# First norm's sums of squares by rows, and the first pair's values in turn with its keys and queries

## The chip, the cores and the metric

The kernel runs on one core of one Trainium2 chip. The metric is the device time of one execution in microseconds (us); the kernel before takes 1274.79 us, the median of three runs from 1274.36 to 1276.12. TensorE is called PE here, VectorE DVE, ScalarE ACT, GpSimd POOL, and SyncE SP; SP issues nearly all DMA transfers and does so in the order of its queue.

## What is computed

One layer of a hybrid encoder trunk on 1024 tokens and 16 learned meta tokens ahead of them, 1040 rows of 1024 features:

```python
def rmsnorm(x, g):
    y = x32 * lax.rsqrt(jnp.mean(x32 * x32, axis=-1, keepdims=True) + EPS)
    return y * g
a = rmsnorm(h, norm1)
proj = a @ w_in                     # pooling input, FoX q/k/v, forget gates, stick-breaking q/k/v
y_pool = multiscale_pool_mixer(u)   # windows 2, 4, 8, 16
y_fox = forgetting_attention(qf, kf, vf, log_f)      # 6 heads of 64, causal softmax with a gate bias
y_sb = stick_breaking_attention(qs, ks, vs)          # 6 heads of 64, strictly causal
h = h + concat(y_pool, y_fox, y_sb) @ w_out
a = rmsnorm(h, norm2)
h = h + (silu(a @ w_gate) * (a @ w_up)) @ w_down
out = rmsnorm(h, final_norm)[16:]
```

All of it is float32. The kernel splits each operand into a high part that PE reads in its fast float32 format and a low part (the rest), and makes three matmuls of each product: high by high, low by high, high by low.

## The kernel before, in words

The head of the program, the first 60 us, is what the change touches. The tokens lie in memory twice: transposed (`xT`, features on the 128 partitions, eight tiles of 1040 tokens) and by rows (`xtok`, used later for the residual).

The loop over the eight tiles (L206) loads a transposed tile, splits it into high and low parts scaled by the norm's gain (L219 on ACT, L220 on DVE), and multiplies it with the first weights: the queries and the keys of the first pair of heads, which add up over the eight tiles in five PSUM buffers ("o" and "s"). The weights come in parts of 128 KB; POOL makes the high part and DVE the low one (L163 to L167). The scale of each token, one over the root of its mean square, isn't known yet; it is multiplied in later, when a product leaves PSUM.

For that scale, `square` (L198) squares each tile on ACT and adds it to an accumulator, on POOL for tiles 1, 3 and 5 and on DVE for the other four. After the loop the accumulator is split, and PE sums it over the partitions with a matrix of ones (L236 to L238), which leaves each token's sum on all partitions at once. ACT makes the scale `rbc` [128, 1040] of it (L242, L244). Two of the three sums lie in the PSUM buffers "mm", of which there are two.

`project_first` then makes the first pair ready: `queries` for both halves of the tokens (scale on DVE at L307, the high part on POOL, its copy to the other half of the partitions on ACT at L314, the low part on DVE at L315), `keys` for three ranges of tokens (L319, a high part on POOL, L327), and last `values`. That is a generator: it loads its weights, and for each of three ranges of tokens makes 24 matmuls into an "mm" buffer (L292), scales the result on DVE (L357), and turns it by PE into another "mm" buffer (`turn`, L343), from which ACT and DVE write the high and low parts (L350, L351). It gives way at two places within the 24 matmuls, at their end, and after each `turn`.

After that the attention of six pairs runs in turn with a stream of filler: the projections of the next pairs, the pooling mixer, and the output projection. The first pair is a stick-breaking one; its scores (L449 to L454) start with the last queries and the last keys, and a softmax-like chain on ACT and DVE follows (L481 to L494).

The order of instructions on each engine is not the written one. A planner simulates the engines and takes what is ready by priority; the written order is the priority, and attention gets 300 places of advance. Buffers of one name are taken in rotation in the written order, so a tile waits for the release of the one that had its buffer before.

Of the kernel before, what the change touches and what calls it, by code (L numbers as in the profile page):

```python
# [8 lines left out]
F32 = mybir.dt.float32  # L9
F32R = mybir.dt.float32r  # L10
BF16 = mybir.dt.bfloat16
AF = mybir.ActivationFunctionType
ALU = mybir.AluOpType
PSUM = bass.MemoryType.PSUM

D = 1024
KD = 8
NM = 16
SEQ = 1024
L = NM + SEQ  # L20
# [3 lines left out]
NB = 9  # L24
T0 = 528
KPIECES = ((0, 264), (264, 264), (528, 512))
# [4 lines left out]
def hymba_trunk(  # L31
# [19 lines left out]
    nc = tc.nc  # L51
    V, S, G, PE = nc.vector, nc.scalar, nc.gpsimd, nc.tensor

    def pool(name, side=None, space=None, bufs=1):
        kw = {}
        if side is not None:
            kw["side"] = side
        if space is not None:
            kw["space"] = space
        return tc.tile_pool(name=name, bufs=bufs, reuse_waits="tile", **kw)  # L60
# [3 lines left out]
    def T(p, shape, dt, tag, bufs=1):  # L64
        uid[0] += 1
        return p.tile(list(shape), dt, tag=tag, bufs=bufs, name=f"{tag}_{uid[0]}")
# [9 lines left out]
    def hi_pool(o, i):  # L76
        G.tensor_scalar(o, i, 1.0, 0.0, ALU.mult, ALU.add)
# [13 lines left out]
    def mm(tag, shape, bufs):  # L91
        return T(ps, shape, F32, tag, bufs)

    MMB, SB_, OB = 2, 4, 2
# [6 lines left out]
    sp_ = st_stack.enter_context(pool("st"))  # L101
# [6 lines left out]
    identr = cst.tile([128, 128], F32R, name="identr")  # L108
# [16 lines left out]
    epst = cst.tile([128, 1], F32, name="epst")  # L125
# [26 lines left out]
    V.tensor_copy(hmean[0:64, 0:64], tmp4[0:64, 0:64])  # L152
    V.tensor_copy(hmean[64:128, 64:128], tmp4[64:128, 64:128])

    ones = T(sp_, [128, 128], F32R, "ones")
    tmp5 = T(sp_, [128, 128], F32, "c3")
    V.memset(tmp5, 1.0)
    V.tensor_copy(ones, tmp5)


    def wpart(c, hf):
        raw = T(r1, [128, 2, 128], F32, "wr", 4)
        nc.sync.dma_start(raw, w_in[c, :, 2 * hf:2 * hf + 2, :])  # L163
        wh = T(r1, [128, 2, 128], F32R, "wh", WB)
        hi_pool(wh, raw)
        wl = T(r1, [128, 2, 128], F32R, "wl", WB)
        WPE[0].tensor_tensor(wl, raw, wh, ALU.subtract)  # L167
        return wh, wl
# [12 lines left out]
    def xhi(k, t0, n):  # L181
        if t0 < T0:
            return xs["h0", k // 2][:, k % 2, t0:t0 + n]
        return xs["h1", k // 2][:, k % 2, t0 - T0:t0 - T0 + n]
# [5 lines left out]

    first_q = [mm("o", [128, 512], OB) for _ in range(2)]
    first_k = [mm("s", [128, 512], SB_) for _ in range(3)]
    sums = [mm("s", [128, 512], SB_)] + [mm("mm", [128, 512], MMB) for _ in range(2)]
    C0 = PAIRS[0][1]
    acc = T(sp_, [128, L], F32, "acc")
    raws = {}

    def square(k):  # L198
        if k == 0:
            S.activation(acc, raws[k], AF.Square)  # L200
            return
        sq = T(sp_, [128, L], F32, "sq", 2)
        S.activation(sq, raws[k], AF.Square)
        (G if k in (1, 3, 5) else V).tensor_tensor(acc, acc, sq, ALU.add)

    for k in range(KD):  # L206
        raws[k] = T(sp_, [128, L], F32, "xr", 4)
        nc.sync.dma_start(raws[k], xT[:, k, :])
        if k % 2 == 0:
            wq = wpart(C0, k // 2)  # L210
            wk = wpart(C0 + 3, k // 2)
        if k % 2 == 0:
            xs["h0", k // 2] = T(x0, [128, 2, T0], F32R, "xa", 4)
            xs["h1", k // 2] = T(hp, [128, 2, 512], F32R, "x1", 8)
            xs["l1", k // 2] = T(hp, [128, 2, 512], F32R, "x1", 8)
        xs["l0", k] = T(x0, [128, T0], F32R, "xb", 8)
        for t0, n in ((0, T0), (T0, 512)):
            rw = raws[k][:, t0:t0 + n]
            S.activation(xhi(k, t0, n), rw, AF.Copy, scale=n1[:, k:k + 1])  # L219
            V.scalar_tensor_tensor(xlo(k, t0, n), rw, n1[:, k:k + 1], xhi(k, t0, n), ALU.mult, ALU.subtract)  # L220
        if k >= 2:
            square(k - 2)
        for ww, xx in ((0, xhi), (0, xlo), (1, xhi)):
            st, sp2 = k == 0 and (ww, xx) == (0, xhi), k == KD - 1 and ww == 1
            for j in range(2):
                PE.matmul(first_q[j], wq[ww][:, k % 2, :], xx(k, NM + 512 * j, 512),
                          start=st, stop=sp2)
            for i, (t0, n) in enumerate(KPIECES):
                PE.matmul(first_k[i][:, :n], wk[ww][:, k % 2, :], xx(k, t0, n), start=st, stop=sp2)
    square(KD - 2)  # L230
    square(KD - 1)
    sqh = T(sp_, [128, L], F32R, "sqh")
    S.copy(sqh, acc)
    sql = T(sp_, [128, L], F32R, "sq", 2)
    V.tensor_tensor(sql, acc, sqh, ALU.subtract)
    for i, (t0, n) in enumerate(KPIECES):  # L236
        PE.matmul(sums[i][:, :n], ones, sqh[:, t0:t0 + n], start=True, stop=False)
        PE.matmul(sums[i][:, :n], ones, sql[:, t0:t0 + n], start=False, stop=True)  # L238

    rbc = T(r1, [128, L], F32, "rbc")  # L240
    for i, (t0, n) in enumerate(KPIECES):
        S.activation(rbc[:, t0:t0 + n], sums[i][:, :n], AF.Ln, scale=1.0 / D, bias=epst[:, 0:1])  # L242
    for t0, n in KPIECES:
        S.activation(rbc[:, t0:t0 + n], rbc[:, t0:t0 + n], AF.Exp, scale=-0.5)  # L244


    csum = T(r1, [128, L], F32R, "csum")
# [57 lines left out]
    def queries(pr, j, p):  # L305
        t = T(at, [128, 512], F32, "pt", 3)
        V.scalar_tensor_tensor(t, p, 0.125, rbc[:, NM + 512 * j:NM + 512 * j + 512], ALU.mult, ALU.mult)  # L307
        first = pr is prs[0]
        for h in range(2):
            a, b = 64 * h, 64 * (1 - h)  # L310
            hi, lo = pr.q1[h][j], pr.q2[h][j]
            zero_r(G, lo[b:b + 64, :])
            hi_pool(hi[a:a + 64, :], t[a:a + 64, :])
            S.copy(hi[b:b + 64, :], t[a:a + 64, :])  # L314
            (V if first or h else G).tensor_tensor(lo[a:a + 64, :], t[a:a + 64, :], hi[a:a + 64, :], ALU.subtract)  # L315

    def keys(pr, t0, n, p):
        t = T(at, [128, 512], F32, "pt", 3)
        V.tensor_tensor(t[:, :n], p[:, :n], rbc[:, t0:t0 + n], ALU.mult)  # L319
        for h in range(2):  # L320
            a, b = 64 * h, 64 * (1 - h)
            src = t[a:a + 64, :n]
            dh = pr.k1[h][a:a + 64, t0:t0 + n]
            dl = pr.k1[h][b:b + 64, t0:t0 + n]
            first = pr is prs[0]
            hi_pool(dh, src)
            (V if first else G).tensor_tensor(dl, src, dh, ALU.subtract)  # L327

    def values(pr, cv):
        w = wload(cv)  # L330
        pr.v = [T(at, [128, NB, 128], F32R, "v", 4) for _ in range(2)]

        for h in range(2):
            zero_r(G, pr.v[h][:, 0, :])

        todo = None

        def turn(t, b0, nb):
            tp = mm("mm", [128, 4, 128], MMB)
            c = 0  # L340
            for i in range(nb):
                m = NM if b0 + i == 0 else 128
                PE.transpose(tp[:m, i, :], t[:, c:c + m], ident)  # L343
                c += m
            for i0, rows, ni in (((0, NM, 1), (1, 128, 2)) if b0 == 0 else ((0, 128, nb),)):
                for h in range(2):
                    src = tp[:rows, i0:i0 + ni, 64 * h:64 * h + 64]
                    dh = pr.v[h][:rows, b0 + i0:b0 + i0 + ni, 64 * h:64 * h + 64]
                    dl = pr.v[h][:rows, b0 + i0:b0 + i0 + ni, 64 - 64 * h:128 - 64 * h]
                    S.copy(dh, src)  # L350
                    V.tensor_tensor(dl, src, dh, ALU.subtract)  # L351

        for t0, n, b0, nb in ((0, NM + 256, 0, 3), (NM + 256, 256, 3, 2), (T0, 512, 5, 4)):
            o = []
            yield from proj_piece(w, t0, n, o)
            t = T(at, [128, 512], F32, "pt", 3)
            V.tensor_tensor(t[:, :n], o[0][:, :n], rbc[:, t0:t0 + n], ALU.mult)  # L357
            if todo is not None:
                turn(*todo)
                yield 0.5  # L360
            todo = (t, b0, nb)
        turn(*todo)
        yield 0.5
# [20 lines left out]
    def project_first(pr, c):  # L384
        forget_weights()
        new_queries(pr)
        for j in (1, 0):
            queries(pr, j, first_q[j])
        new_keys(pr)
        for i, (t0, n) in enumerate(KPIECES):  # L390
            keys(pr, t0, n, first_k[i])
        for _ in values(pr, c + 6):
            pass


# [470 lines left out]
    g = len(OGROUPS) - 1  # L866
# [157 lines left out]
    for c0 in range(2, FF, 2):  # L1024
# [6 lines left out]
        for key, x in up.items():  # L1031
            g = gate[key]
# [61 lines left out]
    for k, (n, direct_, to) in enumerate(DOWN):  # L1094
        ps_ = [mm("s", [128, 512], SB_) if k % 2 == 0 else mm(("mm", "o")[b // 2], [128, 512], 2) for b in range(4)]
        for c0 in range(2, FF, 2):
            x = loaded(lsd[n, c0], "sg")
            if direct_:
                i, dh = direct_
# [91 lines left out]
```

## Time and profile before

| | |
|---|---|
| median of the runs | 1274.79 us |
| profiled execution | 1275.25 us |
| its span, first to last instruction | 1273.5 us |
| busy PE, DVE, ACT, POOL | 95%, 72%, 49%, 38% |
| mean granted clock of PE | 0.987 |
| moved by DMA | 147.12 MB, 116 GB/s on average |

The profile is of one execution. The busy time of an engine is a sum over its instructions; a stage's row says how much of that stage each engine was busy. The granted clock is the share of its full speed that PE was given. In a row of waits, `A <- B` means that an instruction of A sat idle until B was done. In a row of the timeline the first number is the start and the second the duration in us.

### The profile page before, as it was taken

How to read it: one execution, taken by the hardware profiler on the slowest of the kernel's cores; microseconds unless marked ns; L12 is line 12 of the kernel's file. 1: busy time of each engine (PE TensorE's matmuls, PEld its weight loads, DVE VectorE, ACT ScalarE, POOL GpSimd, SP SyncE). 2: the span in 40 equal slices, each digit the busy share in tenths (PEclk: the TensorE clock that was granted, in tenths of full speed). 3: DMA queues.
4: the chain of work that ended last, by engine and by line, in shares of the span. 5: the costliest groups of instructions: out<-in, count | busy, mean ns of one | idle time of the engine just before them, and what ended most of it. 6: DMA issues, size and time to landing. Idle time of an engine off the chain costs nothing.

```text
span 1273.5 us, 18419 instructions
## 1 busy us (share of the span) xinstructions
PE 1214.7 (95%) x6358; PEld 1024.5 (80%) x6358; DVE 916.6 (72%) x1576; ACT 623.6 (49%) x1270; POOL 486.5 (38%) x546
## 2 busy tenths in 40 slices
PE   7799899999999989999999999999999999999997
PEld 5588688889888877787787888888888888788885
DVE  8668975657857678998687676666676646766557
ACT  6466754545538677778644232333232324344443
POOL 6459245463355774440105445334354310000001
PEclk9899999999999999999999999999999999999999
DMA  5100011010101161201514554444554448576653
GB/s 181 42 13 29 15 49 33 30 38 18 51 28 32 38 229 54 75 26 66 190 67 133 190 180 160 147 142 133 190 186 155 153 142 310 170 224 194 194 174 141
DMA packets 73146, 147.12 MB, mean 116 GB/s; under 512 B 9053, under 2 KB 21341, under 8 KB 73053
## 3 DMA queue, kind: packets, MB, share of 16 engines
q1 hardware_dynamic: 69728, 142.01, 33.9%
q10 hardware_dynamic: 3324, 3.95, 0.9%
q8 instruction: 50, 0.82, 0.3%
q14 instruction: 44, 0.35, 0.1%
HBM read 103.98 MB, written 41.94 MB: 115 GB/s over the span
## 4 chain that ended last, share of the span: by engine, by line
PE 70%; DVE 15%; issue 5%; ACT 5%; DMA 3%; POOL 1%; DVEq 0%; SPq 0%; POOLq 0%; ACTq 0%
PE s L901 22%; PE mm L292 12%; PE mm L901 8%; PE s L1086 7%; PE mm L712 4%; PE o L533 4%; DVE r L490 3%; PE s L544 3%; PE o L1086 3%; PE mm L1086 3%; DVE P L492 1%; PE s L449 1%; PE s L451 1%; DVE pl L548 1%; DVE x L714 1%
## 5 line engine op out<-in xcount | busy, mean ns | idle before, releaser
L901 PE MATMUL s<-t,wh 128*128 128x512 f32 x544 | 168.8, 389 | 1.6 <-ACT wh L887 1.6
L901 PEld LDWEIGHTS s<-t,wh 128*128 128x128 f32 x544 | 101.9, 188 | 23.4 <-ACT wh L887 2.2
L901 PE MATMUL s<-s,wh 128*128 128x512 f32 x384 | 118.5, 390 | 0.9 <-ACT wh L887 0.9
L548 DVE TENSOR_TENSOR pl<-s,ph 128x512 fp32r<-128x512 f32 (+1 forms) x168 | 92.3, 569 | 36.3 <-ACT ph L547 32.2
L887 ACT CAST wh<-ss 128x512 fp32r<-128x512 f32 x80 | 49.6, 622 | 127.2 <-PE s L901 92.2
L547 ACT CAST ph<-s 128x512 fp32r<-128x512 f32 (+1 forms) x168 | 79.2, 495 | 60.2 <-PE o L533 32.7
L901 PE MATMUL s<-t,wl 128*128 128x512 f32 x272 | 105.6, 389 | 0.0
L292 PE MATMUL mm<-x,wh 128*128 128x512 f32 (+1 forms) x320 | 100.7, 388 | 0.4 <-DVE pt L357 0.4
L1074 ACT CAST wh<-sg 128x512 fp32r<-128x512 f32 x74 | 46.1, 624 | 108.0 <-PE s L1086 43.0
L901 PE MATMUL mm<-t,wh 128*128 128x512 f32 x320 | 98.6, 389 | 0.0
L1075 DVE TENSOR_TENSOR wl<-sg,wh 128x512 fp32r<-128x512 f32 x74 | 51.1, 691 | 60.4 <-ACT wh L1074 60.2
L887 ACT CAST wh<-raw 128x512 fp32r<-128x512 f32 x68 | 41.8, 622 | 106.0 <-PE s L901 67.3
L544 PE MATMUL s<-identr,P 128*128 128x128 f32 x528 | 81.7, 275 | 6.3 <-DVE pl L548 2.3
L901 PEld LDWEIGHTS s<-s,wh 128*128 128x128 f32 x384 | 72.0, 188 | 16.2 <-ACT wh L887 1.3
L1125 POOL TENSOR_TENSOR r<-r,mhalf 128x1 f32<-128x1 f32 x8 | 4.4, 550 | 210.7 <-DVE r L1124 209.1
L533 PE MATMUL o<-pl,v 128*128 128x256 f32 (+1 forms) x288 | 81.6, 308 | 0.6 <-DVE pl L548 0.6
L995 DVE TENSOR_TENSOR cg<-s,tmp 128x512 f32<-128x512 f32 x60 | 41.3, 688 | 55.5 <-PE s L901 55.4
L292 PE MATMUL mm<-xa,wh 128*128 128x264 f32 (+3 forms) x248 | 77.4, 314 | 1.0 <-ACT rbc L242 0.7
L533 PE MATMUL o<-ph,v 128*128 128x256 f32 (+1 forms) x288 | 76.9, 283 | 0.1
L292 PE MATMUL mm<-xb,wh 128*128 128x264 f32 (+3 forms) x248 | 76.7, 311 | 0.0
L292 PE MATMUL mm<-xa,wl 128*128 128x264 f32 (+3 forms) x248 | 76.4, 312 | 0.0
L544 PEld LDWEIGHTS s<-identr,P 128*128 128x128 f32 x528 | 62.0, 140 | 16.8 <-DVE pl L548 4.5
(290 smaller groups left out, 3574.8 us busy)
## 6 DMA issues: line engine op xcount, KB each, us to landing
sg<-lsd SPq DMA_DIRECT2D x70, 256.0 KB, 3.3
raw<-in_w_gate SPq DMA_DIRECT2D x22, 512.0 KB, 5.3
raw<-in_w_up SPq DMA_DIRECT2D x22, 512.0 KB, 3.7
wr<-in_w_in SPq DMA_DIRECT2D x80, 128.0 KB, 2.2
raw<-in_w_down SPq DMA_DIRECT2D x20, 512.0 KB, 3.6
lsd<-cg SPq DMA_DIRECT2D x40, 256.0 KB, 3.4
raw<-rsd SPq DMA_DIRECT2D x40, 256.0 KB, 3.3
raw<-in_w_down SPq DMA_DIRECT2D x34, 256.0 KB, 3.1
```

The source lines that it names most:

```text
L292: PE.matmul(p[:, :n], w[k][ww], xx(k, t0, n), start=i == 0, stop=i == 23)
L533: PE.matmul(po[:, c:256], pr.v[h][:, kb, :], x, start=first and ix == 0, stop=(kb == nkb - 1 and ix == 1), skip_group_check=True)
L544: PE.transpose(tp[:, 128 * i:128 * i + 128], ptiles[ii][:, k0:k0 + 128], ident)
L547: S.copy(ph[:, :n], tp[:, :n])
L548: V.tensor_tensor(pl[:, :n], tp[:, :n], ph[:, :n], ALU.subtract)
L712: PE.matmul(p, y_[:, ts_], w_[:, ds], start=i == 0, stop=i == 3 * len(ws) - 1)
L887: S.copy(wh, a)
L901: PE.matmul(p, ws[ww][:, k, :], xs_[xx][:, k, :], start=first and i == 0, stop=i == 11, skip_group_check=True)
L995: V.tensor_tensor(t, x, y, ALU.add)
L1074: S.copy(wh, a)
L1075: V.tensor_tensor(wl, a, wh, ALU.subtract)
L1086: PE.matmul(p, x[xx][:, 128 * b:128 * b + 128], y[yy], start=first and i == 0, stop=last and i == 2, skip_group_check=True)
```

## The change

The sums of squares are taken from `xtok` instead. Nine blocks of 128 tokens (the last has 16) are loaded by rows, 512 KB each, through four buffers; ACT squares a block and sums along its rows in one instruction, so that each token's sum is one number on its own partition, in a tile `ssq1` [128, 9]. Rows 0 to 5 are loaded from tile 2 of the loop on, each behind that tile's own load, and the squares follow two tiles later. The scale is made on those nine columns. To spread it over all partitions it is split into a high and a low part, and PE multiplies, for each block, the column broadcast as a weight with the identity: 18 matmuls, into one "s" and two "mm" buffers, and three copies to `rbc`. The matrix of ones, the accumulator and its additions go.

In `project_first` the values no longer come last. A piece of them (three steps of the generator) stands behind the upper queries, behind each of the three key ranges, now from the last to the first, and then come the lower queries and the rest. The high parts of the first pair's keys go from POOL to ACT.

```diff
-    ones = T(sp_, [128, 128], F32R, "ones")
...
-    sums = [mm("s", [128, 512], SB_)] + [mm("mm", [128, 512], MMB) for _ in range(2)]
-    acc = T(sp_, [128, L], F32, "acc")
-    def square(k):
-        if k == 0:
-            S.activation(acc, raws[k], AF.Square)
-            return
-        sq = T(sp_, [128, L], F32, "sq", 2)
-        S.activation(sq, raws[k], AF.Square)
-        (G if k in (1, 3, 5) else V).tensor_tensor(acc, acc, sq, ALU.add)
+    ssq1 = T(sp_, [128, NB], F32, "ssq1")
+    V.memset(ssq1, 1.0)
+    def load_rows(r):
+        n = min(128, L - 128 * r)
+        rows[r] = T(sp_, [128, D], F32, "xk", 4)
+        nc.sync.dma_start(rows[r][:n, :], xtok[128 * r:128 * r + n, :])
+    def square(r):
+        n = min(128, L - 128 * r)
+        S.activation(rows[r][:n, :], rows[r][:n, :], AF.Square, accum_out=ssq1[:n, r:r + 1])
...
         if k >= 2:
-            square(k - 2)
+            load_rows(k - 2)
+        if k >= 4:
+            square(k - 4)
...
-    square(KD - 2)
-    square(KD - 1)
-    sqh = T(sp_, [128, L], F32R, "sqh")
-    S.copy(sqh, acc)
-    sql = T(sp_, [128, L], F32R, "sq", 2)
-    V.tensor_tensor(sql, acc, sqh, ALU.subtract)
-    for i, (t0, n) in enumerate(KPIECES):
-        PE.matmul(sums[i][:, :n], ones, sqh[:, t0:t0 + n], start=True, stop=False)
-        PE.matmul(sums[i][:, :n], ones, sql[:, t0:t0 + n], start=False, stop=True)
+    for r in range(KD - 4, NB):
+        if r >= KD - 2:
+            load_rows(r)
+        square(r)
+    S.activation(ssq1, ssq1, AF.Ln, scale=1.0 / D, bias=epst[:, 0:1])
+    S.activation(ssq1, ssq1, AF.Exp, scale=-0.5)
+    rrh = T(sp_, [128, NB], F32R, "rrh")
+    V.tensor_copy(rrh, ssq1)
+    rrl = T(sp_, [128, NB], F32R, "rrl")
+    V.tensor_tensor(rrl, ssq1, rrh, ALU.subtract)
     rbc = T(r1, [128, L], F32, "rbc")
-    for i, (t0, n) in enumerate(KPIECES):
-        S.activation(rbc[:, t0:t0 + n], sums[i][:, :n], AF.Ln, scale=1.0 / D, bias=epst[:, 0:1])
-    for t0, n in KPIECES:
-        S.activation(rbc[:, t0:t0 + n], rbc[:, t0:t0 + n], AF.Exp, scale=-0.5)
+    for g in range(3):
+        p = mm("s", [128, 512], SB_) if g == 0 else mm("mm", [128, 512], MMB)
+        blocks = range(4 * g, min(4 * g + 4, NB))
+        for r in blocks:
+            n = min(128, L - 128 * r)
+            c = 128 * (r - 4 * g)
+            for x in (rrh, rrl):
+                PE.matmul(p[:, c:c + n], x[:, r:r + 1].to_broadcast([128, 128]), identr[:, :n],
+                          start=x is rrh, stop=x is rrl, skip_group_check=True)
+        n = c + n
+        (S.copy if g != 1 else V.tensor_copy)(rbc[:, 512 * g:512 * g + n], p[:, :n])
...
-            hi_pool(dh, src)
+            (S.copy if first else hi_pool)(dh, src)
...
     def project_first(pr, c):
         forget_weights()
         new_queries(pr)
-        for j in (1, 0):
-            queries(pr, j, first_q[j])
         new_keys(pr)
-        for i, (t0, n) in enumerate(KPIECES):
-            keys(pr, t0, n, first_k[i])
-        for _ in values(pr, c + 6):
+        vals = values(pr, c + 6)
+
+        def piece():
+            for _ in range(3):
+                next(vals, None)
+
+        queries(pr, 1, first_q[1])
+        piece()
+        for i in (2, 1, 0):
+            keys(pr, *KPIECES[i], first_k[i])
+            piece()
+        queries(pr, 0, first_q[0])
+        for _ in vals:
             pass
```

More of the change, by code (lines that the diff above doesn't have):

```diff
@@ L153, in hymba_trunk @@
     V.tensor_copy(hmean[64:128, 64:128], tmp4[64:128, 64:128])
-    ones = T(sp_, [128, 128], F32R, "ones")
-    tmp5 = T(sp_, [128, 128], F32, "c3")
-    V.memset(tmp5, 1.0)
-    V.tensor_copy(ones, tmp5)
     def wpart(c, hf):
@@ L192, in hymba_trunk @@
     first_k = [mm("s", [128, 512], SB_) for _ in range(3)]
-    sums = [mm("s", [128, 512], SB_)] + [mm("mm", [128, 512], MMB) for _ in range(2)]
     C0 = PAIRS[0][1]
-    acc = T(sp_, [128, L], F32, "acc")
-    raws = {}
-    def square(k):
-        if k == 0:
-            S.activation(acc, raws[k], AF.Square)
-            return
-        sq = T(sp_, [128, L], F32, "sq", 2)
-        S.activation(sq, raws[k], AF.Square)
-        (G if k in (1, 3, 5) else V).tensor_tensor(acc, acc, sq, ALU.add)
+    ssq1 = T(sp_, [128, NB], F32, "ssq1")
+    V.memset(ssq1, 1.0)
+    raws, rows = {}, {}
+    def load_rows(r):
[5 more added lines that the diff above has]
+        S.activation(rows[r][:n, :], rows[r][:n, :], AF.Square, accum_out=ssq1[:n, r:r + 1])
     for k in range(KD):
```

## The prediction, made before the result

> **What bounds the kernel now.** I read the page's busy times first, then busy time by stage, then who waited for whom on TensorE (PE), and last the timeline of the first 60 us, since every edit lies there.
>
> ```profile
> span 1273.5 us, 18419 instructions
> PE 1214.7 (95%) x6358; PEld 1024.5 (80%) x6358; DVE 916.6 (72%) x1576; ACT 623.6 (49%) x1270; POOL 486.5 (38%) x546
> ```
>
> PE is busy for 1214.7 of 1273.5 us, so 59 us is all that reordering can win. The next view cuts the span where PE's work changes: the first queries and keys (to 34.82), the norm (to 39.84), the first two value pieces (to 47.46), a hole (to 50.70), the third value piece (to 57.26), and then attention. Columns: length, then busy time and instruction count of PE, PE's weight load, DVE, ACT and POOL, then the granted clock, DMA share and GB/s.
>
> ```profile
> 0.00:34.82 34.82, 25.36 (x119) 21.18 (x120) 30.36 (x45) 19.60 (x25) 21.73 (x40) 1.00 0.54 173
> 34.82:39.84 5.02, 1.89 (x10) 0.94 (x8) 3.08 (x4) 2.06 (x4) 2.36 (x3) 1.00 0.19 58
> 39.84:47.46 7.62, 7.61 (x48) 7.40 (x48) 5.89 (x9) 4.05 (x8) 4.76 (x7) 0.78 0.10 32
> 47.46:50.70 3.24, 0.00 (x1) 0.01 (x1) 3.08 (x7) 0.00 (x0) 1.57 (x3) 0.93 0.00 0
> 50.70:57.26 6.56, 6.56 (x25) 5.38 (x25) 2.84 (x7) 0.94 (x4) 3.50 (x7) 0.78 0.07 21
> 57.26:70.00 12.74, 9.88 (x58) 8.54 (x57) 10.10 (x18) 9.29 (x22) 1.70 (x3) 0.87 0.10 32
> 70.00:140.00 70.00, 65.64 (x416) 55.74 (x415) 53.79 (x93) 47.27 (x109) 49.52 (x54) 1.00 0.08 24
> 500.00:1273.50 773.50, 754.23 (x3437) 620.60 (x3435) 551.17 (x788) 325.26 (x588) 213.54 (x161) 0.99 0.47 154
> ```
>
> From 70 us on PE is busy for 65.64 of 70 and later 754.23 of 773.5: work that reaches PE earlier in the head ends earlier at the end. In the head PE loses 9.5 us in the first stage, 3.1 in the norm, 3.2 in the hole, 2.9 in early attention; and the clock of 0.78 in two stages costs 0.22 x 7.62 = 1.7 and 0.22 x 6.56 = 1.4 us more. PE's own waits (total us, times, longest):
>
> ```profile
> PE o L226 <- POOL wh L77: 7.3, 1, 7.3
> PE mm L343 <- DVE pt L357: 3.8, 2, 3.3
> PE s L449 <- DVE P L492: 2.3, 1, 2.3
> PE o L226 <- DVE xb L220: 2.0, 1, 2.0
> PE s L237 <- ACT sqh L233: 1.4, 1, 1.4
> PE s L238 <- DVE sq L235: 1.1, 1, 1.1
> PE mm L292 <- ACT rbc L242: 0.7, 1, 0.7
> ```
>
> The first is the load of the first weights and stays. The 2.0, and the 1.4 + 1.1 + 0.7 = 3.2 of the norm, and the hole (3.3) are what the change touches. The timeline shows why DVE was late for the 2.0 (start, duration):
>
> ```profile
> 18.20 2.53 POOL L204 TENSOR_TENSOR acc<-acc,sq 128x1040 f32<-128x1040 f32 x1 [2.27 <-DVE c L157]
> 18.39 2.92 DVE L220 SCALAR_TENSOR_TENSOR xb<-xr,n,xa 128x528 fp32r<-128x528 f32 x1
> 22.03 0.76 DVE L220 SCALAR_TENSOR_TENSOR xb<-xr,n,xa 128x528 fp32r<-128x528 f32 x1
> ```
>
> The same DVE instruction takes 0.76 us alone and 2.92 beside POOL's addition of squares: it stands still until POOL is done.
>
> **What goes, and what DVE gets back.**
>
> ```profile
> L204 POOL TENSOR_TENSOR acc<-acc,sq 128x1040 f32<-128x1040 f32 x3 | 8.2, 2742 | 4.8 <-ACT x L219 2.5 <-DVE c L157 2.3
> L204 DVE TENSOR_TENSOR acc<-acc,sq 128x1040 f32<-128x1040 f32 x4 | 4.9, 1232 | 0.0
> ```
>
> Gone are four DVE additions (4.9 us), the three POOL additions with up to 2.92 - 0.76 = 2.2 us of stall each on DVE (some 6.5), the copy and split of the accumulator, six matmuls and six wide ACT passes. DVE was busy for 30.4 of 34.8 us and loses about 11. Then PE's own work sets the first stage: it ends 2.0 + 0.2 us earlier, at about 33 rather than 35.2. That does not by itself move anything: the value matmuls need two PSUM buffers ("mm") that the norm holds first, before and after.
>
> **What comes instead: when the last row lands.** Nine loads by rows join SP's queue, 8 x 0.524 + 0.066 = 4.26 MB, as much as the eight transposed tiles (8 x 0.532 = 4.26) beside 1.05 MB of first weights. In all 9.6 MB must land. What DMA gave:
>
> ```profile
> 2.00:14.00 12.00, 6.74 (x23) 5.74 (x24) 8.67 (x13) 8.63 (x14) 9.80 (x21) 1.00 0.98 318
> 14.00:30.00 16.00, 13.99 (x75) 11.69 (x73) 15.96 (x23) 8.71 (x13) 8.41 (x9) 1.00 0.38 118
> xr<-in_xT SPq DMA_DIRECT2D x8, 520.0 KB, 4.5
> ```
>
> Full, it moves 318 GB/s; from 14 us it stood at 0.38, because tiles came free late. If it stays full from 2 us, 9.6/0.318 = 30.2 us: the last row lands at 32.2, or 33.8 if the 0.5 MB of value weights slip ahead. The queue order lets it stay nearly full: SP can have four transposed tiles and four rows under way; row 4 waits for the square of row 0, written after tile 4's copies, and so on to row 7, which waits for the square of row 3, after tile 7's copies. Tile 7 lands at 2 + 7.9/0.318 = 27, its copies and square 3 end at about 29.5; row 7, issued then, lands about 4 us later (4.5 is the median under load). I take **33 us** for the last row. Behind the waiting rows in SP's in-order queue stand tile 7 (needed by PE at about 30, so there with 3 us to spare) and the value weights (needed at 40). Bounds: 31 (row 7 issued with tile 7's landing, 4 us more) and 40.6 (after 14 us only the mean of the two rates, 218 GB/s, for the remaining 5.8 MB).
>
> [...] The trace's own 318 over 12 full microseconds is used here.
>
> **From the last row to the value matmuls.** The nearest rows for the new small steps:
>
> ```profile
> L737 ACT ACTIVATE xa<-x x8: 1042/1054/1062, 591.6 to 627.5; 128x1024 f32<-128x1024 f32 x8
> L737 ACT ACTIVATION_READ_ACCUMULATOR xa<-x x8: 183/186/192, 592.5 to 628.4; 128x1 f32 x8
> L739 ACT ACTIVATE r<-ssq,epst x4: 280/291/297, 592.8 to 603.4; 128x1 f32<-128x1 f32 x4
> L740 ACT ACTIVATE r<-r x4: 199/203/206, 593.1 to 603.7; 128x1 f32<-128x1 f32 x4
> L1124 DVE TENSOR_SCALAR r<-ssq x7: 144/144/148, 1250.5 to 1266.1; 128x1 f32<-128x1 f32 x7
> 96.51 0.44 PE s L544 x4
> ```
>
> A square with its sum is 1.05 + 0.19 = 1.24 us; ACT has room for nine (11 us; it was busy for 19.6 of 34.8, of which 8 x 1.06 squares go). After the last row: two squares less the 0.2 between the two landings, 2.2; Ln and Exp on nine columns 0.5; two tiny DVE steps 0.3; handovers 0.4: 3.4 us. Then 18 matmuls with 128 moving columns, of which 16 lie before the second group's copy: at 0.11 each (four transposes in 0.44) 1.8, at half clock 3.6; I take 2.7. The copy out of PSUM is 0.7 (512 columns, DVE) plus a handover, 0.8. Value matmuls start at 33.0 + 3.4 + 2.7 + 0.8 = **39.9**; before:
>
> ```profile
> 39.84 0.43 PE L292 MATMUL mm<-xa,wh 128*128 128x272 f32 x1 [0.68 <-ACT rbc L242]
> 41.45 1.29 DVE L307 SCALAR_TENSOR_TENSOR pt<-o,rbc 128x512 f32<-128x512 f32 x2 [2.75 <-ACT rbc L244]
> 50.20 0.77 DVE L357 TENSOR_TENSOR pt<-mm,rbc 128x272 f32<-128x272 f32 x2
> 57.26 0.37 PE L449 MATMUL s<-k,q 128*128 128x456 f32 x1
> ```
>
> So this term is +0.1, between -2 (row at 31) and +7.6 (row at 40.6). The scales are then complete for queries too, against 41.45.
>
> **The clock in the first two pieces.** Now 0.78, a loss of 1.7. The 3.2 us of pauses ahead of it brought half clock for some 3.5 us:
>
> ```profile
> 40.00:42.00 2.00, 2.00 (x10) 2.00 (x10) 0.55 (x1) 1.42 (x4) 0.00 (x0) 0.50 0.32 103
> 42.00:44.00 2.00, 2.00 (x13) 2.00 (x12) 2.00 (x4) 1.78 (x3) 1.61 (x3) 0.65 0.00 0
> ```
>
> After, PE pauses once, from 33 to 36.4, and then the small broadcasts take the slow time. Term: -1.0, between 0 and -1.7.
>
> [...]
>
> **The value pieces in turn.** Now both evacuations wait until 50.20 on DVE, behind both query halves and the keys, though PE had ended both pieces by 47.46. After, the written order sets evacuation 0 after the upper queries and last keys, evacuation 1 after the middle keys. DVE from 39.9: scale 0.65, keys 0.69, two query subtractions 0.93 each, two of the keys 0.8 each, 4.8 in all: 44.7 plus handovers to ACT and POOL, about 45.5, for evacuation 0, while PE works on piece 1 until 46.5. Then keys 264 wide, 1.4 us, and evacuation 1 at about 47.2; with 0.4 for it the third piece starts 1.1 us after the second ends, against 3.24. Term: -2.1, between 0 and -3.2. The six key copies that go from POOL to ACT cost ACT 4 x 0.38 + 2 x 0.62 = 2.8 us by these rows, where it was busy for 4.05 of 7.62 us and then not at all; the cover is ample, and 2.8 us is their price without it.
>
> ```profile
> L350 ACT CAST v<-mm 128x256 fp32r<-128x256 f32 x2 | 0.8, 376 | 0.0
> L314 ACT CAST q<-pt 64x512 fp32r<-64x512 f32 x4 | 2.5, 619 | 0.8 <-DVE pt L307 0.8
> ```
>
>
> **The clock behind the hole.** The 3.24 us hole is followed by 0.78, a loss of 1.4. The 2.0 us pause at 19.4 brought no slow stretch (the first stage shows 1.00). With a pause of 1.1 it goes: -1.2, between 0 and -1.4.
>
> **Sum.** 0.1 - 1.0 - 2.1 - 1.2 = -4.2 us. The profiled execution took 1275.25 us (1273.5 and 1.75 around it), 0.46 above the median of 1274.79. So 1271.05 for such an execution and **1270.6** for a median. What a measurement of this kernel tells from no change is 0.2%, 2.55 us.
>
> **The rivals.**
>
> *Early attention moves up too* (1267.6).
>
> ```profile
> 51.00 1.60 DVE L327 TENSOR_TENSOR k<-pt,k 64x512 fp32r<-64x512 f32 x2
> ```
>
> Scores started at 57.26, though the last key part was split by 52.6. The keys and upper queries would be ready at 47 or so, and the third piece would cover part of the softmax chain that PE waits for now (2.3 on L492, and the 0.87 clock after it, 1.6). Another 3 us goes. Against it: the planner put the scores behind the third piece before, and may do so again.
>
> *The gain is handed back* (1274). What is written in turn is only a priority; if the planner leaves DVE's order, the hole and its clock stay, and only about -0.8 is left. Or the hole only moves to L492's wait, since DVE is busy for 10.1 of the 12.7 us after 57.26. For: in that stage DVE, not PE, is the fuller. Against: the six POOL copies ahead of the key subtractions go to ACT.
>
> *The rows come late* (1278.2). One mechanism: SP's in-order queue stops on a row whose buffer is not free, DMA runs at a mean of 218 GB/s after 14 us, the last row lands at 40.6 and value matmuls start at 47.5. That is +7.6 in place of +0.1, -4.2 becomes +3.4. It decides from 37.2 (no gain left) and is slower by 0.2% from 39.8. For: the 0.38 of 14 to 30 us was just such waiting. Against: what held the tiles then was DVE beside POOL, which goes.
>
> **How the numbers follow.** Forecast 0.42, early attention too 0.18, handed back 0.23, late rows 0.17. So faster 0.60, within 0.2% 0.23, slower 0.17. The range goes from the forecast with row 31 and early attention (-9 to -10) to the late rows' price: 1265 to 1278; the forecast's own range is 1267 to 1272.2.
>
> **What would show it.** No DVE instruction of 2.9 us before 33; DMA share above 0.9 from 2 to 30 us; the last square's sum at about 35; value matmuls from about 40; the first value evacuation at 45 to 46 and a pause under 1.5 us ahead of the third piece at full clock. It would be wrong if the last sum comes after 39, if PE waits on tiles before 33, or if the first scores come earlier by several us and the end doesn't follow.

## The result

The changed kernel takes 1277.93 us, the median of 16 runs (1274.86 to 1282.42); the kernel before took 1274.97 beside it (16 runs, 1273.08 to 1277.46). The ratio is 1.0023, with a 95% interval from 1.0013 to 1.0033: some 3 us slower, where 4.2 us faster were forecast. The profiled execution of the changed kernel is one of its quickest, 1275.61 us with a span of 1273.8, 0.36 us above that of before. So there are two things to explain: where the 4.2 us went, which the two traces can show, and why the median lies 2.3 us above the execution that was profiled.

The page of the changed kernel, its span and busy times:

```profile
span 1273.8 us, 18454 instructions
PE 1214.1 (95%) x6370; PEld 1027.3 (81%) x6370; DVE 904.7 (71%) x1573; ACT 625.1 (49%) x1283; POOL 469.2 (37%) x537
```

DVE lost 11.9 us of work and POOL 17.3, as the change says. PE has as much work as before (1214.7 then) and as much idle time.

**The head went better than forecast.** Busy time by stretch of the changed kernel (length, then PE, weight load, DVE, ACT and POOL with their counts, granted clock, DMA share, GB/s):

```profile
2.00:14.00 12.00, 6.79 (x21) 5.71 (x22) 8.57 (x17) 6.45 (x11) 7.83 (x20) 1.00 0.96 341
14.00:30.00 16.00, 16.00 (x87) 13.74 (x86) 9.80 (x20) 12.38 (x21) 2.91 (x6) 1.00 1.00 381
30.00:40.00 10.00, 8.26 (x49) 7.45 (x49) 4.53 (x9) 5.53 (x12) 3.64 (x6) 0.86 0.19 57
40.00:50.00 10.00, 10.00 (x62) 8.84 (x61) 7.50 (x16) 4.59 (x12) 3.16 (x5) 0.97 0.06 16
50.00:60.00 10.00, 6.16 (x37) 5.62 (x36) 7.54 (x15) 7.58 (x19) 3.87 (x6) 0.88 0.13 39
```

From 14 to 30 us PE is never idle (13.99 of 16 before) and the DMA engines are full at 381 GB/s, where they had stood at 0.38 and 118. From 50 to 60, though, PE is busy for only 6.16 us. The waits of PE from 7 to 75 us (total, times, longest) say what for:

```profile
PE o L225 <- POOL wh L77: 7.2, 1, 7.2
PE mm L299 <- DVE v L358: 3.8, 1, 3.8
PE s L248 <- DVE rrh L237: 1.4, 1, 1.4
PE mm L299 <- ACT rbc L251: 0.4, 1, 0.4
```

The 2.0 us wait on DVE's tiles, the 3.3 us hole and the 2.3 us wait of the first scores are gone. A new wait of 3.8 stands in their place. The timeline shows the steps in order (start, duration):

```profile
31.58 1.04 ACT L201 ACTIVATE xk<-xk 16x1024 f32<-16x1024 f32 x1
32.42 0.39 PE L228 MATMUL s<-x,wl 128*128 128x512 f32 x1
32.75 0.30 ACT L234 ACTIVATE ssq<-ssq,epst 128x9 f32<-128x9 f32 x1
34.20 0.33 PE L248 MATMUL s<-identr,rrh 128*128 128x128 f32 x1 [1.38 <-DVE rrh L237]
36.72 0.36 PE L299 MATMUL mm<-xa,wh 128*128 128x272 f32 x1 [0.35 <-ACT rbc L251]
44.31 0.42 DVE L364 TENSOR_TENSOR pt<-mm,rbc 128x256 f32<-128x256 f32 x1 [0.22 <-PE mm L299]
44.35 0.46 PE L465 MATMUL s<-k,q 128*128 128x456 f32 x1
44.90 0.71 PE L299 MATMUL mm<-x,wh 128*128 128x512 f32 x2
53.56 0.28 DVE L358 TENSOR_TENSOR v<-mm,v 128x128 fp32r<-128x128 f32 x1
54.15 0.69 DVE L322 TENSOR_TENSOR q<-pt,q 64x512 fp32r<-64x512 f32 x1 [0.32 <-POOL q L77]
55.73 0.84 DVE L358 TENSOR_TENSOR v<-mm,v 128x256 fp32r<-128x256 f32 x2 [0.89 <-ACT v L357]
56.72 0.36 PE L299 MATMUL mm<-xa,wh 128*128 128x264 f32 x1 [3.84 <-DVE v L358]
```

Value matmuls start at 36.72 instead of 39.84, the first scores at 44.35 instead of 57.26, and the third value piece starts at 44.90 with no pause ahead of it. Then the matmuls of 56.72 wait until the low part of the values is written, and on DVE the lower queries' low part (L322, 54.15) stands ahead of that.

**Where it is lost.** The starts of the same ACT instructions were set against each other in both traces (lines that run equally often in both); each figure is the median of after less before, in us, for instructions that start in that stretch of the kernel before:

```
stretch before   60-80  120-160  217-330  440-465  600-640  700-900  1100-1250  end of span
after            -5.9    -7.0     -4.5     -4.4     +0.5     +2.7      +0.4       +0.4
```

The changed kernel is ahead by 4.5 us from 217 to 465 us, nearly the 4.2 that were forecast, and has lost all of it by 600. What lies between is the last pair's attention, the pooling mixer's rest and the output projection, none of which the change touches. What differs is the order: in the two programs as built, the order on PE, DVE and ACT agrees from about 180 to 460 us; from 468 us on it differs in 65 places on PE, 28 on DVE and 51 on ACT, until the output projection is over. The planner, starting from another head, has dealt the tail anew. PE's waits in that stretch, first of before from 460 to 640 us, then of after from 456 to 640:

```profile
PE mm L712 <- DVE x L714: 3.6, 5, 1.4
PE mm L712 <- DVE v L351: 2.8, 1, 2.8
PE s L449 <- DVE P L492: 1.0, 1, 1.0
PE s L755 <- ACT xa L744: 0.9, 1, 0.9
...
PE s L544 <- DVE P L492: 0.2, 1, 0.2
```

```profile
PE mm L728 <- DVE x L730: 5.5, 7, 1.6
PE mm L728 <- DVE v L358: 2.8, 1, 2.8
PE s L560 <- DVE P L508: 2.2, 2, 1.8
PE s L771 <- ACT xa L760: 1.7, 1, 1.7
PE s L465 <- DVE P L508: 1.3, 2, 1.0
```

The residual additions of the output projection (L714, now L730) come late seven times instead of five, and the softmax chain (L492, now L508) holds PE for 3.5 us instead of 1.0 + 0.2. Cut at the same matmuls of PE (937 in each), the whole stretch reads like this, before and after:

```profile
455.00:640.00 185.00, 173.93 (x937) 141.99 (x937) 157.86 (x268) 134.73 (x296) 66.43 (x68) 0.99 0.30 104
```

```profile
450.60:640.50 189.90, 174.87 (x937) 142.98 (x937) 157.39 (x267) 133.92 (x296) 66.23 (x68) 0.98 0.29 102
```

It is 4.9 us longer, from -4.4 to +0.5. PE is idle for 189.90 - 174.87 = 15.0 us of it, 11.1 before: 4.0 us are waits. The rest is the clock. A stretch at a granted clock of 0.50 follows the 2.8 us pause in both (466.66 to 470.07 in before, 460.46 to 467.29 in after), with PE busy for 3.41 us of it in before and for 5.71 in after, and half of the difference is 1.1 us. That part does not go with the order: in the table below half clock costs the tail 1.7 us in old_sbc70 and turn_alone, with the order of after, and 3.0 in values_last, with that of before.

**Half-clock stretches.** In these two traces stretches at half clock follow pauses of PE: single ones of 1.8 to 3.8 us (in before 3.25 at 47.45 and 1.78 at 1085.21, in after 3.84 at 52.87 and 2.47 at 669.18) or several shorter ones. The 2.01 us pause of before at 19.36 and the 1.88 us one of after at 117.33 had none behind them (clock 1.00 from 19 to 24 and from 117 to 127). In both traces each stretch is 3.41 us long or twice that (6.83), but for the last, which the end of the execution cuts off; the clock in it is 0.50, so 3.41 us of it with PE busy cost 1.7 us. Behind the tail, before has one at 1087.9 us that after has not, and after has one at 672.1. Before, then after:

```profile
1086.00:1092.00 6.00, 5.01 (x15) 4.00 (x16) 4.71 (x9) 1.86 (x3) 0.00 (x0) 0.72 0.67 210
```

```profile
670.00:676.00 6.00, 4.34 (x12) 3.33 (x13) 4.37 (x5) 3.69 (x7) 4.70 (x4) 0.72 0.00 0
```

They make 1.7 of the 2.2 us by which after falls back further from 600-640 to 700-900, and take 1.7 back before the end. They also bear on the median. The mean granted clock of a whole execution is 0.987 in the median of the runs of before (those beside the experiments, for which it is known) and 0.984 in those of after, so PE gave up 0.013 x 1273.5 = 16.6 us there and 0.016 x 1276.2 = 20.4 here. Over the 16 runs of after the time goes with the clock given up (0.77 us for each us, correlation 0.79). The profiled execution had 0.986. So the extra 2 us of the median go with 0.002 x 1276.2 = 2.6 us more of clock given up; at 1.7 us each that would be one more half-clock stretch or two, an estimate from these numbers. What stands ahead of them in the other runs can't be seen, since those left no trace.

### The profile page after: what moved, and what is told of

The parts are those of the page before. It is cut to its first block, busy times and chain, and to the rows that moved or that the text cites. A ratio compares the mean times of both kernels' runs of the same rounds, so it can differ in the third digit from the quotient of the medians.

```text
span 1273.8 us, 18454 instructions
## 1 busy us (share of the span) xinstructions
PE 1214.1 (95%) x6370; PEld 1027.3 (81%) x6370; DVE 904.7 (71%) x1573; ACT 625.1 (49%) x1283; POOL 469.2 (37%) x537
## 4 chain that ended last, share of the span: by engine, by line
PE 70%; DVE 14%; issue 6%; ACT 4%; DMA 4%; POOL 1%; SPq 0%; DVEq 0%; POOLq 0%; ACTq 0%
PE s L917 22%; PE mm L299 12%; PE mm L917 8%; PE s L1102 7%; PE mm L728 4%; DVE r L506 4%; PE o L549 4%; PE s L560 3%; PE mm L1102 3%; PE o L1102 3%; PE s L465 2%; PE s L467 1%; DVE P L508 1%; DMA wr<-in_w_in 1%; DVE pl L564 1%
## 5 line engine op out<-in xcount | busy, mean ns | idle before, releaser
L299 PE MATMUL mm<-x,wh 128*128 128x512 f32 (+1 forms) x320 | 97.8, 379 | 0.4 <-DVE pt L364 0.4
```

The lines of the kernel that those rows point to most:

```text
L299: PE.matmul(p[:, :n], w[k][ww], xx(k, t0, n), start=i == 0, stop=i == 23)
```

## The experiments

Two theories stood against each other. **Tail**: the head is worth its 4 us, and the new order from 468 us on throws it away; with the new head and the old tail's order the kernel is faster than before. **Head**: the head's gain is only shifted and is lost again wherever PE waits for other engines, whatever the order. The expectations also name two forms of the second: **clock** (the head's new pauses bring more half clock later) and **resource** (more DMA, later weights). What each kernel did, in the same table as above. The column tail is the change from 440-465 to 600-640. The last two are measured like the 15.0 us above, between the same matmuls: idle time of PE, and what half clock cost it.

```
              60-80  120-160  217-330  440-465  600-640  end    tail   idle  clock
before                                                                 11.1    1.7
after          -5.9    -7.0     -4.5     -4.4     +0.5   +0.4   +4.9   15.0    2.9
new_sbc70      -6.2    -7.5     -7.0     -7.0     -6.6   -6.5   +0.4   11.0    1.7
old_sbc70      +0.9    +0.9     -1.3     -1.3     +2.1   +4.4   +3.4   15.6    1.7
old_sbc75      +1.4    +0.8     +7.9     +7.9    +13.0  +12.7   +5.1   15.6    2.9
new_fgs2       -6.4    -7.1     -7.2     -5.0     -4.8   -5.3   +0.2   10.9    1.5
rows_fgs2      -8.7    -2.3     -5.2     -5.0     -4.9   -2.6   +0.1   11.0    1.4
rows_alone     -8.7    -4.3     -3.2     -1.7     +0.3   +0.4   +2.0   14.2    1.7
turn_alone     -1.3    +6.4     +6.2     +6.2    +10.0  +10.5   +3.8   15.4    1.7
values_last   -11.4    +4.3     +2.6     +2.6     +3.9   +5.2   +1.3   11.1    3.0
```

The tail's order as built is that of before in new_sbc70, new_fgs2, rows_fgs2 and values_last; it is that of after in old_sbc75 and, up to about 612 us, in turn_alone and old_sbc70; rows_alone has one of its own. The table stands on one execution of each kernel, in which a half-clock stretch more or less shifts a figure by 1.7 us; those of old_sbc75 and values_last were the slowest of their runs.

**The old tail's order behind the new head.** `SBC` is the weight with which a stick-breaking pair's attention is dealt out among the filler (times 0.7 for the last pair). At 70 the planner gives the changed kernel the head of after, nearly its middle, and the tail of before.

```diff
-    SBC, FOXC = 65.0, 38.0
+    SBC, FOXC = 70.0, 38.0
```

> The changed kernel with one planning weight (SBC, the attention's share in the written order) at 70 instead of 65. The built program has the same order as the changed kernel in the head, nearly the same in the middle, and from the last pair of heads on, on every engine, the order of the kernel before. Tail theory (the head's gain of 4.4 us reaches 460 us and is lost because the planner put the last pair and the output projection in another order): 1270.5 us, 4 to 5 under before. Clock theory (the head's new pauses bring more half-clock windows later): the pauses are the same, so about 1278, as the changed kernel. Theory of a resource (more DMA, later weights): about 1278 too.

Measured: 1269.12 us (6 runs, 1268.5 to 1270.87) beside 1276.11 for before on the same chip, ratio 0.9949 (0.9934 to 0.9964). The tail theory had 1270.5, the others about 1278. It is the fastest of all kernels tried. The output projection's squares, eight of a line that the prediction showed for before (591.6 to 627.5), in after and in this one:

```profile
L753 ACT ACTIVATE xa<-x x8: 1040/1058/1062, 590.0 to 627.0; 128x1024 f32<-128x1024 f32 x8
```

```profile
L753 ACT ACTIVATE xa<-x x8: 1042/1056/1065, 585.0 to 620.8; 128x1024 f32<-128x1024 f32 x8
```

And PE's waits from 454 to 634 us:

```profile
PE mm L728 <- DVE x L730: 3.6, 5, 1.4
PE mm L728 <- DVE v L358: 2.8, 1, 2.8
PE s L771 <- ACT xa L760: 0.9, 1, 0.9
PE s L560 <- DVE pl L564: 0.8, 2, 0.5
```

The rows are those of before (3.6 in five, 2.8, 0.9), and the lead of 7.0 us at 465 is 6.6 at 640: a head that is ahead does carry through when the tail keeps its order. In two stretches of the tail after and this kernel stand like this:

```profile
490.00:510.00 20.00, 17.35 (x88) 13.52 (x87) 17.81 (x30) 12.67 (x29) 10.79 (x10) 1.00 0.16 48
570.00:590.00 20.00, 17.00 (x116) 14.79 (x115) 18.05 (x39) 15.13 (x42) 1.24 (x2) 1.00 0.00 1
```

```profile
487.00:507.00 20.00, 18.40 (x95) 14.65 (x94) 18.79 (x32) 15.52 (x34) 9.91 (x10) 1.00 0.15 45
567.00:587.00 20.00, 19.09 (x117) 15.57 (x116) 17.30 (x38) 14.96 (x43) 1.24 (x2) 1.00 0.06 26
```

PE gets 1.05 and 2.09 us more work done in 20 us each, at the same clock. Not all of this kernel's gain is the tail, though: from 160 to 330 us it keeps 2.5 us that after gives up. There its order is not quite that of after (on PE between about 130 and 180 us), and the clock differs. The stretch from 145 to 171 us of before, after and this kernel:

```profile
145.00:171.00 26.00, 20.66 (x135) 18.13 (x135) 22.82 (x54) 16.80 (x40) 9.30 (x16) 0.93 0.13 40
```

```profile
145.00:171.00 26.00, 21.33 (x119) 18.71 (x118) 20.98 (x57) 15.29 (x36) 9.30 (x18) 0.80 0.15 46
```

```profile
145.00:171.00 26.00, 23.42 (x160) 20.52 (x159) 23.07 (x64) 16.24 (x39) 9.80 (x21) 0.93 0.15 46
```

After has three half-clock stretches in it, the two others one; two more cost (0.93 - 0.80) x 26 = 3.4 us of clock. The new kernel has another just ahead (granted clock 0.89 from 130 to 145 us, 0.11 x 15 = 1.7 us, where after has 1.00), so against it the clock accounts for 1.7 of the 2.5 us.

**The weight alone.** The same number in the kernel before, and 75, which gives the kernel before the tail's order of after:

> The kernel before with the planning weight at 70, the same number that brings the changed kernel to 1269. The head is the old one, the middle differs little, the tail is in yet another order, close to that of the changed kernel. If the weight itself saves time, 1270 to 1272. By the tail theory it only deals another order: 1276 to 1280, and the loss lies behind 460 us.

> The kernel before with the same weight at 75: the head is the old one instruction for instruction, the middle is ordered somewhat differently, and from the last pair on the order is that of the changed kernel. Tail theory: slower than before by about the 4.9 us that the tail lost, 1280. Clock or resource theory: the head's pauses and loads are the old ones, so 1275 within 1.

With 70: 1281.34 us (5 runs, 1278.56 to 1284.49) beside 1275.09, ratio 1.0049 (1.0028 to 1.0070). With 75: 1285.87 (6 runs, 1284.27 to 1288.06) beside 1276.11, ratio 1.0082 (1.0066 to 1.0098). The first lies 1.3 us above the 1276 to 1280 that the tail theory gave. So 70 is no better weight by itself: on the old head it costs 0.5%, on the new one it gains 0.5%. The 75 shows the tail's order of after behind the old head, and it loses 5.1 us between 465 and 600, as after does (4.9). It also lost 7 us before, between 160 and 217 us, which was not expected: 1280 had been written down. Most of that is the clock: from 152 to 187 us it has 17.1 us of half clock, before 3.4. Over the whole profiled execution its mean clock was 0.982, so 0.018 x 1286.2 = 23.2 us were given up, against the 16.6 of before.

**The tail's order brought back another way.** `FGS` says after how many steps of the second pair's projection the forget gates are put in.

```diff
-    FGS = 4
+    FGS = 2
```

> The changed kernel with one other planning number: the forget gates stand after the third step of the second pair's projection instead of the fifth (FGS 2 for 4). From the last pair on its order is that of the kernel before, and the middle, from 100 to 460 us, is nearly that of the kernel before as well. Tail theory: about 4.5 us ahead at 460 us, and still 4 to 4.5 ahead at 640 us; 1270.5 to 1271.5, granted clock 0.987. If the gain of the weight at 70 came from that weight and not from the order of the tail, this one lands at 1277 to 1278.

> Only the sums of squares by rows, with the forget gates two steps earlier, which gives the order of the kernel before from the last pair on. Against the run of rows alone (about 1.5 over before; a third order of the tail, which lost 2 us) the tail should lose nothing: by the tail theory lag at 640 us equals lag at 460 us within 0.5. The lag at 460 us itself depends on the middle's order; between -4 and 0, so 1271 to 1275.

The changed kernel with it: 1271.92 us (12 runs, 1269.7 to 1275.77) beside 1275.09, ratio 0.9977 (0.9964 to 0.9989). The part by rows alone with it: 1272.87 (10 runs, 1269.67 to 1276.93), ratio 0.9980 (0.9964 to 0.9995). The first had been put at 1270.5 to 1271.5, the second at 1271 to 1275. Both have the tail of before and lose 0.2 and 0.1 us in it. With another knob the answer is the same, so it is the order and not the weight.

**The parts by themselves.** The sums by rows without the values in turn (`rows_alone`), and the values in turn with the old sums (`turn_alone`):

```diff
-            (S.copy if first else hi_pool)(dh, src)
+            hi_pool(dh, src)
...
-        vals = values(pr, c + 6)
-        queries(pr, 1, first_q[1])
-        piece()
...
+        for j in (1, 0):
+            queries(pr, j, first_q[j])
+        for i, (t0, n) in enumerate(KPIECES):
+            keys(pr, t0, n, first_k[i])
+        for _ in values(pr, c + 6):
+            pass
```

The diff is that of `rows_alone` against the changed kernel; `turn_alone` is the kernel before with these lines reversed.

> Only the sums of squares by rows; values last and the first keys on POOL, as before. Value matmuls start at about 37 as in the changed kernel (39.8 before), but the 3 us hole ahead of the third value piece stays. If the two parts add up, it is some 2 us ahead of before at 180 us and the whole 4.5 us come from both. Its tail is in a third order: the end may lie 2 us under before or up to 3 over by the tail theory.

> Only the values in turn and the first keys on ACT; the norm as before. Its tail has the changed kernel's order. Value matmuls start at 39.8 as before, the hole is gone: 2 to 2.5 us ahead at 180 us. Tail theory: that is lost and more, 1277 to 1278. Clock or resource theory (extra loads hurt): 1272 to 1273, since nothing is loaded twice.

Rows alone: 1277.96 us (10 runs, 1270.29 to 1280.39), ratio 1.0013 (0.9996 to 1.0029), no change that can be told. It leads by 8.7 us at 60 to 80, more than the whole change, and loses it step by step, 2.0 of it in a tail order of its own. The values in turn alone: 1287.95 (4 runs, 1285.7 to 1288.51), ratio 1.0097 (1.0076 to 1.0118), 10 us above what was expected. It has lost 6 us by 120 to 160. PE's longest waits ahead of that, from 60 to 130:

```profile
PE s L458 <- DVE P L501: 7.9, 2, 4.1
```

Scores wait for the softmax chain of DVE, twice for some 4 us. Half clock comes on top: 17.1 us of it from 60 to 125 us, where before has 3.4; the granted clock was 0.74 from 57 to 70 us and 0.75 from 120 to 130, in before 0.87 and 1.00. That DVE comes late because of the old norm, so that attention which starts early only waits there, is argued and not shown. The two parts don't add: +0.13% and +0.97% against +0.23% together.

**The turn taken back.** To price the turn alone behind the new norm, the values went last again, everything else of the change left as it is:

```diff
-        def piece():
-            for _ in range(3):
+        def piece(n):
+            for _ in range(n):
                 next(vals, None)
...
-        piece()
-        for i in (2, 1, 0):
+        piece(0)
+        for i, n in ((2, 0), (1, 0), (0, 0)):
```

> The changed kernel with the values made last again (rows, keys from the last to the first range, key copies on ACT stay). Its order from the last pair on is that of the kernel before, its middle differs from both. By the prediction's step on values in turn, the hole of about 3 us ahead of the third value piece is back and it is about 2 to 3 us behind the changed kernel at 60 us; that the tail keeps everything, so the end is 1271 to 1274. If the values in turn are worth nothing it ends at 1269 to 1271.

Measured: 1278.61 us (10 runs, 1274.76 to 1280.41), ratio 1.0020 (1.0007 to 1.0033); expected were 1271 to 1274. It led by 11.4 us at 60 to 80 and was 4.3 behind at 120 to 160. PE's waits from 34 to 140 us, and the stretch in which the lead goes:

```profile
PE s L465 <- DVE P L508: 7.2, 6, 2.6
PE s L560 <- DVE P L508: 2.8, 1, 2.8
```

```profile
100.00:140.00 40.00, 30.16 (x155) 24.93 (x153) 29.37 (x41) 21.80 (x52) 26.98 (x29) 0.87 0.09 27
```

The hole that was expected ahead of the third value piece did not come back: the first scores, at 45.15 us, stand there. So this kernel does not price the turn; it shows once more that the order behind an edit decides. Its tail, in before's order, lost 1.3 us, and half clock cost it 3.0 us there, against 1.7 in before.

**What follows.** In the four kernels whose tail has the order of before, PE is idle there for 10.9 to 11.1 us, as in before (11.1); in the four with the order of after, wholly or up to 612 us, for 15.0 to 15.6; in rows_alone for 14.2. In time the tail costs 0.1 to 1.3 us against before in the first, 3.4 to 5.1 in the second and 2.0 in the last; in old_sbc70 and rows_alone the matmuls themselves take about 1 us less. The tail theory stands on these nine. The head theory is contradicted by new_sbc70, new_fgs2 and rows_fgs2, with the new sums in their head, and by old_sbc75, which has the old head and loses as much. Left open are which input of the planner turns the tail's order, what the turn alone is worth, and what stands ahead of the half-clock stretches of the runs that were not profiled.

## Why the prediction was wrong

**The step that failed** is the reading of the first view: "work that reaches PE earlier in the head ends earlier at the end". It took the order behind the head as given. The lead was there (4.4 us at 440 to 465), and the tail took 4.9: 4.0 in waits that the new order brought, and about 1.1 of half clock. A busy PE of 754.23 in 773.5 us does not say that the rest is the same work in the same order: PE's idle time in the tail, 11.1 us, became 15.0. The last sentence of the prediction named this outcome ("the first scores come earlier by several us and the end doesn't follow"), but none of its rivals had it as a cause: "The gain is handed back" put the return into the head, and the late rows, the only slower case, did not happen.

**The clock in the median.** No term of the sum was for the half-clock stretches outside the head. By the clock of the 16 runs (0.984 in the median, 0.986 in the profiled one) they are what puts the median 2.3 us above the profiled execution, in which after and before are equal within 0.4 us; without traces of the other runs this is argued and not shown.

**The terms of the head**, one by one.

- *First stage ends at about 33.* Its last matmul ends at 32.42 + 0.39 = 32.8. Right. DVE's slowest splits now:

```profile
L217 DVE SCALAR_TENSOR_TENSOR xb<-xr,n,xa x8: 757/769/900, 6.0 to 25.4; 128x528 fp32r<-128x528 f32 x8
```

  No 2.9 us instruction is left, at most 0.90. In before each of the three POOL additions (2.53 to 2.87 us, at 11.35, 18.20 and 27.04) had one DVE instruction of 2.46 to 2.92 us beside it, which ended 0.1 to 0.6 us after it; so the stall was rightly read.
- *Last row at 33, value matmuls at 39.9 (+0.1).* Too late. The last square starts at 31.58 and Ln at 32.75, where 35 was forecast. Two rates were too low: the DMA moved 341 GB/s to 14 us and 381 to 30, against the 318 that were used; and the 18 broadcasts ran from 34.20 to about 36.2 at full clock, 2.0 us and not 2.7. PE stood for only 1.4 us, not 3.4. The last full row had landed by 30.5, where the 33 stood for it. Value matmuls start at 36.72: the term measured -3.1, 1.1 us past its lower bound of -2.
- *Clock in the first two pieces (-1.0).* The half-clock stretch now lies at 37.2 to 40.6 (granted clock 0.50), on the first piece and not on the broadcasts (1.00 from 34.2 to 36.2): about 0. The pauses ahead of it are 1.4 and 0.4 us, with small matmuls between them.
- *The hole (-2.1 to 1.1 us left).* It is gone altogether: the third piece follows the second at 44.90. The term was -3.2, its lower bound.
- *Clock behind the hole (-1.2).* Right for the third piece (0.97 from 40 to 50), but a half-clock stretch follows the new 3.8 us wait, from 57.7 to 61.1 (0.50), so it is only moved.
- *Early attention moves up (a rival with 0.18).* It did, by 12.9 us. But the 3 us that the rival gave it did not come on top: PE then waits 3.8 us on the values' low part, and the lead at 60 to 80 us is 5.9, no more than the other terms add up to.

Together the four terms measure -3.1 + 0 - 3.2 + 0 = -6.3 by the places at which they were forecast, and the lead at 60 to 80 us is 5.9. So the head was under-estimated, by 2 us; that 4.5 was left at 217 goes with the clock of 145 to 171 us, shown above. That this is close to the forecast's 4.2 is luck.

## What to carry to other kernels

When a planner orders the work by simulated times, an edit in one place can change the order hundreds of microseconds on; before an edit is credited with its time, set the two built orders side by side, and follow the lead of the same instruction through both traces to the place where it is lost. Here the head was 4.4 us ahead at 465 us (7.0 with the nearest other order), and the tail's new order cost 4.0 in waits; the nearest knob of the planner (a weight from 65 to 70) gave 0.5% with the new head and cost 0.5% with the old. So knobs that were set for the old kernel are to be set again after an edit, and a part measured by itself may say nothing of its share in the whole.

## What the runs showed of the hardware that was not expected

One core's DMA held 381 GB/s over 16 us (14 to 30 us of after, share 1.00), above the 318 seen in the head before; before itself had it elsewhere, which the prediction had not looked up:

```profile
460.00:470.00 10.00, 7.07 (x30) 5.43 (x31) 7.02 (x16) 9.55 (x25) 3.64 (x5) 0.83 0.98 384
```

The half-clock stretches of before and after are 3.41 us long, or 6.83 once in after, and the same pause had one unit of 3.41 behind it in the one and two in the other. The matmul that ends the 2.81 us pause in the tail, in before and in after:

```profile
466.02 4.59 PE L712 MATMUL mm<-xa,xb 128*128 128x512 f32 x12 [2.81 <-DVE v L351]
```

```profile
461.58 5.46 PE L728 MATMUL mm<-xa,xb 128*128 128x512 f32 x12 [2.81 <-DVE v L358]
```

The pause is the same to 0.01 us, and half clock lasts from 466.7 to 470.1 in the one and from 460.5 to 467.3 in the other. So the same 12 matmuls took 4.59 us and 5.46. In values_last, whose tail has the order of before, they took as long as in after, behind the same pause:

```profile
468.62 5.46 PE L728 MATMUL mm<-xa,xb 128*128 128x512 f32 x12 [2.81 <-DVE v L358]
```

In each of the two traces all half-clock stretches start whole multiples of 3.413 us apart: in before the second and third, at 50.2 and 63.9, lie 3 and 7 of them behind the first, at 40.0, and in after those at 57.7 and 460.5 lie 6 and 124 behind the first, at 37.2. Why one unit follows in the one and two in the other is not shown. By values_last and by the costs of half clock in the table (1.7 us in old_sbc70 and turn_alone, with the order of after) the second unit in the tail of after does not go with the order. That the wider spread of the changed kernel's runs (7.6 us, against 4.4 before) comes from this is argued and not shown.
